# Sums' loads on SP in the order of use, steps that make sums placed anew, and two places of the first feed-forward moved

## The chip, the cores and the metric

The kernel runs on one core of one Trainium2 chip. The metric is the device time of one execution in microseconds. Three runs of the kernel before took 800.18, 800.39 and 802.68 us; the median is 800.39 us. A separate execution was profiled; its own time was 802.45 us, of which the profile's span covers 800.6 us.

## The reference

One residual block over 256 tokens of width 1024, in float32:

```
x = x + 0.5 * rmsnorm(swiglu(rmsnorm(x), ffn1))            # D_FF = 2816
h = rmsnorm(x); project h to q, forget, input, output gate (HGRN2), q, k, v, forget (FoX), 2 gates
A = gated linear recurrence (8 heads);  B = forgetting attention (8 heads)
x = x + rmsnorm((gate_A * (A @ w_a) + gate_B * (B @ w_b)) @ w_out)
x = x + rmsnorm(cross attention of x with 256 memory tokens, 4 heads of 256)
x = x + 0.5 * rmsnorm(swiglu(rmsnorm(x), ffn2))
```

with `swiglu(h) = (silu(h @ w_gate) * (h @ w_up)) @ w_down`. All weights are read once from HBM.

## The kernel before

**Number format.** A float32 operand is split into two parts, hi (a cast to the matmul's float32r format) and lo (the rest), and a product is made of three matmuls: hi by hi, hi by lo, lo by hi. So each weight unit, a tile of 128 x 1024 (512 KB), goes through three queues: a load into one of 4 "raw" buffers, issued by SP (line 137); a cast on ScalarE (ACT, line 138); and a subtraction on VectorE (DVE, line 139). The results lie in 8 "hi" and 8 "lo" buffers until TensorE (PE, line 94) has used them. Other splits go through the helper `split` (lines 157 and 158).

**Order.** The work is written in program order, and a scheduler, whose own estimate of durations is part of the toolchain, gives each engine one fixed order. `after(i)` puts instructions behind the i-th matmul of the list `log`, with high priority; `tc.issue_after(ins)` puts what follows behind `ins` on that engine. Each engine, and SP and GpSimd (POOL) as issuers of DMAs, works through its order one by one: an instruction that waits holds all behind it.

**Feed-forward.** The 2816 hidden columns are 11 chunks of 256 (gate and up together 512 columns wide). Most chunks are made by `act_tok`, 24 matmuls for each half h of 128 tokens. Pairs of chunks at 5 and 8 (first feed-forward) and at 3, 5, 7 and 9 (second) are made by `quad`, a Strassen-like scheme: seven products of half-size blocks in place of eight, which needs sums of blocks of tokens and sums of blocks of weights. `mixed` makes the tokens' sums once for each feed-forward: it adds hi and lo, multiplies with a row of norms (a small matmul behind the last one in `log`, then ACT), splits the product, makes four sums (line 291) and splits these. `down(c, h)` applies w_down to a chunk's activations; `flush` transposes these activations on TensorE ahead of it.

**Sums of weights.** In the first feed-forward `quad` makes them itself (lines 481 to 494). For the second one they are made ahead, during the middle part of the kernel, in 16 steps. A step loads two units (1 MB) into a "wide" buffer by POOL's queue (`load_step`, line 754), makes four sums in place on DVE (`at`, lines 766 to 769), and stores them to a DRAM tensor `sums` by POOL's queue (line 771), after which it loads the next step but one. `SUMS_AT` says behind which stage of the program each step stands; `TO_GATES` is the number of steps that are loaded before the branch gates, which take one of the wide buffers for themselves for a time. There are 2 wide buffers, and they are the same ones into which `sum_of` of the second feed-forward loads finished sums through SP's queue (line 450).

**Middle part.** The stages in order: `i_a`, `f_a`, `q_a`, output gate with FoX forget, `k_b` and `q_b` (the recurrence's levels run beside these), `v_b`, `gates` 0 to 3, `br_a` and `br_b`, `w_out`, `mk`, `mq`, values `mem_v(0)`, the scores and the softmax of the memory attention (lines 1244 to 1264; the transposes of p are line 1264), `mem_v(1)`, `mo`.

Of the kernel before, what the change touches and what calls it, by code (L numbers as in the profile page):

```python
# [31 lines left out]
L_ACT = 21  # L32
# [21 lines left out]
L_MX = 30  # L54

SUMS_AT = (
    ("i_a", 0), ("f_a", 0), ("f_a", 1), ("q_a", 0), ("q_a", 1), ("q_b", 0), ("q_b", 1), ("gates", 2),
    ("br_a", 0), ("br_b", 0), ("br_a", 1), ("br_b", 1), ("mk", 2), ("mk", 3), ("mq", 0), ("mq", 1),
)
TO_GATES = 7  # L60

_ORDER = [
    ("f1_in", 4 * NFF), ("f1_dn", 2 * NFF),
# [5 lines left out]
_AT = {}  # L71
# [8 lines left out]
def block_kernel(ctx: ExitStack, tc: tile.TileContext, wts, head_in, gf_in, x_in, mem_in, memT_in, cols, rows, fbias, masks, out):  # L80
    nc = tc.nc
    V, S, G, PE = nc.vector, nc.scalar, nc.gpsimd, nc.tensor
# [37 lines left out]
    def trp():  # L120
        return pp.tile([P, 512], F32, tag="tr", name=nm("tr"), bufs=2)
# [3 lines left out]
    loads = []  # L125
# [255 lines left out]
    def ffn(w_in, w_dn, X, r2, n_tok, i_row, quads, sums, first_half, second_half=None):  # L381
# [5 lines left out]
        def flush(n):  # L387

            if late:
                c = late.pop(0)  # L390
                tr = trp()
                trv = tr.rearrange("p (j t) -> p j t", j=2)
                with after(n):
                    for h in range(2):
                        for j in range(2):
                            PE.transpose(trv[:, j, h * P : (h + 1) * P], ats[c, h][:, j * P : (j + 1) * P], ident)  # L396
                    split(acts[c][:, 0], acts[c][:, 1], trv)
# [30 lines left out]
        def quad(c, n_down):  # L428
# [12 lines left out]
            if sums:  # L441
                for i in range(4):
                    hi, lo = load_split(wts[_AT[w_in] + 4 * c + i - 4])
                    B11.append((hi[:, :512], lo[:, :512]))
                    B21.append((hi[:, 512:], lo[:, 512:]))

                def sum_of(k):
                    W = wp.tile([P, 2, D], F32, tag="wide", name=nm("wide"), bufs=2)
                    for q in range(2):
                        loads.append(nc.sync.dma_start(W[:, q], sums[c][(0, 3, 2, 1)[k], q]).ins)  # L450
                    return two(W[:, 0].rearrange("p (i n) -> p i n", i=2)) + two(W[:, 1].rearrange("p (i n) -> p i n", i=2))

                def lower():
                    out = []
                    for q in range(2):
                        u = _AT[w_in] + 4 * c + 2 * q
                        raw = wp.tile([P, D], F32, tag="raw", name=nm("raw"), bufs=4).rearrange("p (i n) -> p i n", i=2)
                        loads.append(nc.sync.dma_start(raw, wts[u : u + 2, :, 512:].rearrange("i p n -> p i n")).ins)
                        out += two(raw)
                    return out  # L460

                summed = None
            else:
                wide, made = [], [[], [], []]
                for q in range(2):
                    W = wp.tile([P, 2, 2, 512], F32, tag="wide", name=nm("wide"), bufs=2)
                    raws = []
                    for i in range(2):
                        u = _AT[w_in] + 4 * c + 2 * q + i
                        raw = wp.tile([P, D], F32, tag="raw", name=nm("raw"), bufs=4)  # L470
                        loads.append(nc.sync.dma_start(raw, wts[u - 4]).ins)
                        loads.append(nc.sync.dma_start(W[:, i].rearrange("p j n -> p (j n)"), wts[u]).ins)
                        hi, lo = parts_of()
                        split(hi, lo, raw)
                        B11.append((hi[:, :512], lo[:, :512]))
                        B21.append((hi[:, 512:], lo[:, 512:]))
                        raws.append(raw)
                    wide.append(W)
                    t1, t2, t4 = (m4([P, 2, 512], n="sum") for _ in range(3))
                    for i in range(2):  # L480
                        V.tensor_tensor(out=t1[:, i], in0=raws[i][:, :512], in1=W[:, i, 0], op=ALU.add)
                    V.tensor_tensor(out=t2, in0=t1, in1=W[:, :, 1], op=ALU.add)
                    for i in range(2):
                        summed = V.tensor_tensor(out=t4[:, i], in0=t2[:, i], in1=raws[i][:, 512:], op=ALU.add).ins
                    for k, t in zip((0, 1, 2), (t1, t2, t4)):
                        made[k].append(t)

                def sum_of(k):
                    if k != 2:
                        t = made[min(k, 2)]  # L490
                        return two(t[0]) + two(t[1])
                    out = []
                    for W in wide:
                        V.tensor_tensor(out=W[:, :, 0], in0=W[:, :, 0], in1=W[:, :, 1], op=ALU.add)  # L494
                        out += two(W[:, :, 0])
                    return out

                def lower():
                    return two(wide[0][:, :, 1]) + two(wide[1][:, :, 1])
# [27 lines left out]
            n = len(log)  # L527
# [18 lines left out]
            n = len(log)  # L546
# [8 lines left out]
            n = len(log)  # L555
# [15 lines left out]
            n = len(log)  # L571
# [50 lines left out]
        for c in range(n_tok, NFF):  # L622
            if c in acts:
                continue
            if c in quads:
                quad(c, done)
                done += 2
                continue
            acts[c] = m4([P, 2, 2, T], F32R, "act")
            if quads and c == quads[0] - 1 and c == 2:  # L630
                ready = mixed(X, r2, L_MX)
            if c == 2 and first_half:
                n = len(log)
                outs = act_first(c, mm)
                for h in range(2):
                    flush(n + L_ACT + 24 * h)
                    act_evac(outs[h], c, h)
            else:
                for h in range(2):
                    n = len(log)  # L640
                    act_tok(c, h)
                    if c == 2 or c > NFF - STAG + 1 or c - 2 in quads:
                        flush(n + L_ACT)
            if c == NFF - 1:
                flush(n + L_ACT)
            if quads and c == quads[0] - 3:
                ready = mixed(X, r2)
            if quads and c == max(2, quads[0] - 2):
                mix.append(ready)
                X = ready[0]  # L650
            if grow is None and c >= quads[0] - 1:
                grow = load_row(i_row)
                if first_half:
                    with tc.issue_after(loads[-1]):
                        nc.sync.dma_start(masks_s, masks)
            if accs is None:
                accs = [[acc(), acc()], [acc(), acc()]]
            while done < min(c - 1, NFF - STAG):
                n = len(log)
                for h in range(2):  # L660
                    down(done, h)
                if c + 1 not in quads:
                    flush(n + L_ACT)
                done += 1
# [64 lines left out]
    def half(X, r, h, g, *ms):  # L729

        for i, m in enumerate(ms):
            with after(m):
                to_T(X, x_blocks(h), h, g, (i,) if len(ms) == 2 else (0, 1))
        r[h] = rstd_x(x_halves(h))
# [9 lines left out]
    sums = {c: dp.tile([4, 2, P, D], F32, name=f"sums_{c}") for c in QUADS_2}  # L744
    steps = [(c, q, i) for c in QUADS_2 for q in range(2) for i in range(2)]
    slots = []
    brows = []

    def load_step():
        if len(slots) < len(steps) and (brows or len(slots) < TO_GATES):  # L750
            c, q, i = steps[len(slots)]
            W = wp.tile([P, 2, 2, 512], F32, tag="wide", name=nm("wide"), bufs=2)
            for e in range(2):
                G.dma_start(W[:, e].rearrange("p j n -> p (j n)"), wts[_AT["f2_in"] + 4 * (c + e - 1) + 2 * q + i])
            slots.append(W)

    def at(name, c=0):
# [13 lines left out]
            G.dma_start(sums[u][2 * e : 2 * e + 2, q, :, i * 512 : i * 512 + 512].rearrange("k p n -> p k n"), W[:, e])  # L771
        load_step()

    for _ in range(2):
        load_step()

    iv = [m4([P, 2, 512], n="iv") for _ in range(2)]
    for h in range(2):
        m = len(log)
        for c in range(2):  # L780
            ps = mm()
            proj_tok(ps, X2, chunk("i_a", c), h)
            iv_last = S.activation(iv[c][:, h, :], ps, AF.Copy, scale=r2[h]).ins
        if h == 0:
            half(X2, r2, 1, G_MIX, m + L_IA)
        at("i_a", h)
    row2 = row_of(r2)

# [18 lines left out]
    for c in range(2):  # L807
        u = chunk("f_a", c)
        f, k = m4([P, 4, T], n="f"), m4([P, 4, T], n="k")
# [12 lines left out]
    for c in range(2):  # L822
        u = chunk("q_a", c)
        q = m4([P, 4, T], n="q")
# [111 lines left out]
    for c in range(3):  # L936
        u = [load_split(gf_in[4 * c + i], GF) for i in range(4)]
        n = min(GF, D - c * GF)
# [59 lines left out]
    for h in range(2):  # L998
        ps = [acc(), acc()]
        for hd in range(8):  # L1000
            g, i = hd // 4, hd % 4
# [239 lines left out]
    for h in range(2):  # L1241
# [14 lines left out]
        p = m4([P, 4, T], n="pm")  # L1256
# [140 lines left out]
```

## Time and profile before

| | |
|---|---|
| median of three runs | 800.39 us |
| profiled execution, its own time | 802.45 us |
| its span | 800.6 us |
| TensorE busy | 778.9 us, 97% |
| VectorE busy | 646.0 us, 81% |
| ScalarE busy | 470.2 us, 59% |
| GpSimd busy | 50.1 us, 6% |
| moved by DMA | 193.61 MB, mean 242 GB/s |

How to read the lines below: times are microseconds from the span's start. PE is TensorE's matmul, PEld its weight load, SPq the queue of DMAs that SP issues. `L94` is a line of the kernel; since `MM` records every matmul, they all have that line, and the tiles tell them apart, as `out<-in`: `mm<-hi,hT` is a product of a weight's hi part with the tokens' hi part, `raw<-in_wts_dram` the load of a weight unit, `wide<-in_wts_dram` a step's load, `sums<-wide` its store, `wide<-sums` the load of finished sums. A bracket at the end of a time line's row is the idle time of that engine just before, and what ended it. A row of the waits reads: waiting engine, tile and line, what it waited for, us in total, how often, the longest. A matmul's busy time overlaps with the next one's, so the distance between starts is the rate.

### The profile page before, as it was taken

To read this page: it belongs to the slowest core of one execution; us is meant where nothing else is said; L and a number is where in the kernel's file an instruction comes from. 1 tells how busy PE (TensorE), PEld (TensorE's weight loads), DVE (VectorE), ACT (ScalarE), POOL (GpSimd) and SP (SyncE) were. 2 spreads that over 40 slices of the span, in tenths; PEclk is the share of its full clock that TensorE was granted. 3 is DMA by queue.
4 is the path that set the end of the run, shared out by engine and by line. 5 is a ranking of instruction groups with operands and counts; after the bars stand their busy time and mean duration, and the time that the engine had idled before them with its cause. 6 is when DMAs were issued, how large, how long until landed. Compare 5 with 4: busy or idle time off the path is not lost.

```text
span 800.6 us, 13165 instructions
## 1 busy us (share of the span) xinstructions
PE 778.9 (97%) x5004; PEld 671.3 (84%) x5004; DVE 646.0 (81%) x1004; ACT 470.2 (59%) x704; POOL 50.1 (6%) x85
## 2 busy tenths in 40 slices
PE   9999999999999999999999999999599999999995
PEld 7878888878899989998888888998488888888884
DVE  6898989868788998599686887976566999978864
ACT  7655664656753447249674345652556758777753
POOL 0000000100112200210001211022000000000000
PEclk9999999999999999999999999999799999999998
DMA  9766474674679964865579998578834269989831
GB/s 350 248 220 239 167 289 141 241 249 158 246 254 323 315 228 126 320 208 190 166 263 343 340 353 310 166 254 300 326 118 161 90 204 313 363 309 313 310 106 53
DMA packets 57391, 193.61 MB, mean 242 GB/s; under 512 B 6248, under 2 KB 9712, under 8 KB 57328
## 3 DMA queue, kind: packets, MB, share of 16 engines
q1 hardware_dynamic: 47504, 157.50, 57.4%
q0 software_dynamic: 9680, 35.14, 11.9%
q8 instruction: 39, 0.64, 0.3%
q14 instruction: 24, 0.20, 0.1%
q10 hardware_dynamic: 144, 0.13, 0.0%
HBM read 174.92 MB, written 17.83 MB: 241 GB/s over the span
## 4 chain that ended last, share of the span: by engine, by line
PE 77%; DMA 9%; DVE 8%; ACT 3%; issue 2%; POOL 0%; DVEq 0%; ACTq 0%; POOLq 0%; SPq 0%
PE mm L94 47%; PE acc L94 24%; DMA raw<-in_wts_dram 5%; PE tr L94 3%; DVE lo L139 3%; DMA sums<-wide 2%; ACT hi L138 2%; PE tr L396 1%; PE tr L316 1%; DMA wide<-in_wts_dram 1%; DMA head<-in_head_dram 0%; ACT hT L157 0%; DVE lT L158 0%; PE tr L1264 0%; ACT junk L244 0%
## 5 line engine op out<-in xcount | busy, mean ns | idle before, releaser
L139 DVE TENSOR_TENSOR lo<-raw,hi 128x1024 fp32r<-128x1024 f32 (+1 forms) x228 | 271.0, 1202 | 65.8 <-ACT hi L138 61.6
L138 ACT CAST hi<-raw 128x1024 fp32r<-128x1024 f32 (+1 forms) x228 | 232.8, 1036 | 141.8 <-PE mm L94 67.6
L94 PE MATMUL mm<-hi,hT 128*128 128x512 f32 (+1 forms) x448 | 171.7, 387 | 0.5 <-DVE G L944 0.4
L94 PE MATMUL mm<-lo,hT 128*128 128x512 f32 (+1 forms) x448 | 171.8, 387 | 0.0
L94 PE MATMUL mm<-hi,lT 128*128 128x512 f32 (+1 forms) x448 | 171.4, 387 | 0.0
L94 PE MATMUL acc<-hi,act 128*128 128x512 f32 x352 | 113.2, 391 | 0.7 <-ACT act L157 0.6
L94 PE MATMUL mm<-hT,hi 128*128 128x256 f32 x384 | 109.0, 284 | 0.6 <-DVE zf L946 0.6
L94 PE MATMUL mm<-hT,lo 128*128 128x256 f32 x384 | 109.0, 284 | 0.0
L94 PE MATMUL mm<-lT,hi 128*128 128x256 f32 x384 | 108.9, 284 | 0.0
L94 PEld LDWEIGHTS mm<-hi,hT 128*128 128x128 f32 x448 | 84.7, 189 | 17.2 <-ACT hT L272 0.7
L94 PEld LDWEIGHTS mm<-hi,lT 128*128 128x128 f32 x448 | 84.5, 189 | 15.9 <-DVE lT L273 0.5
L94 PEld LDWEIGHTS mm<-lo,hT 128*128 128x128 f32 x448 | 84.4, 189 | 14.7
L94 PEld LDWEIGHTS acc<-hi,act 128*128 128x128 f32 x352 | 66.0, 188 | 15.3 <-ACT act L157 1.2
L94 PEld LDWEIGHTS mm<-hT,hi 128*128 128x128 f32 x384 | 73.6, 192 | 0.9 <-ACT hi L138 0.8
L94 PEld LDWEIGHTS mm<-lT,hi 128*128 128x128 f32 x384 | 73.6, 192 | 0.2
L94 PEld LDWEIGHTS mm<-hT,lo 128*128 128x128 f32 x384 | 73.6, 192 | 0.1
L94 PE MATMUL acc<-lo,act 128*128 128x512 f32 x176 | 69.2, 393 | 1.3 <-DVE lo L139 1.3
L158 DVE TENSOR_TENSOR lo<-wide,hi 128x1024 fp32r<-128x1024 f32 x40 | 47.7, 1220 | 3.5 <-ACT hi L157 2.9
L157 ACT CAST hi<-wide 128x1024 fp32r<-128x1024 f32 x40 | 41.8, 1053 | 12.2 <-DVE wide L494 3.4
L94 PEld LDWEIGHTS acc<-lo,act 128*128 128x128 f32 x176 | 33.1, 188 | 8.3 <-DVE lo L139 1.8
L771 POOL DMA_DIRECT2D sums<-wide x32 | 23.5, 734 | 243.7 <-DVE wide L768 222.3
L94 PE MATMUL mm<-hi,sh 128*128 128x512 f32 x96 | 37.5, 390 | 0.0
(243 smaller groups left out, 1130.7 us busy)
## 6 DMA issues: line engine op xcount, KB each, us to landing
raw<-in_wts_dram SPq DMA_DIRECT2D x232, 512.0 KB, 4.7
wide<-in_wts_dram POOLq DMA_DIRECT2D x32, 512.0 KB, 6.7
sums<-wide POOLq DMA_DIRECT2D x32, 512.0 KB, 6.1
wide<-sums SPq DMA_DIRECT2D x32, 512.0 KB, 6.0
raw<-in_gf_dram SPq DMA_DIRECT2D x12, 344.0 KB, 4.8
wide<-in_wts_dram SPq DMA_DIRECT2D x8, 512.0 KB, 6.5
head<-in_head_dram SPq DMA_DIRECT2D x8, 388.0 KB, 5.7
grow<-in_rows_dram SPq DMA_DIRECT2D x4, 512.0 KB, 6.1
```

The lines of the kernel that those rows point to most:

```text
L94: log.append(PE.matmul(*args, **kw).ins)
L138: S.copy(h, r)
L139: V.tensor_tensor(out=l, in0=r, in1=h.bitcast(F32), op=ALU.subtract)
L157: S.copy(hi, src)
L158: V.tensor_tensor(out=lo, in0=src, in1=hi.bitcast(F32), op=ALU.subtract)
L316: PE.transpose(ps[:, j * P : (j + 1) * P], src(kb), ident)
L396: PE.transpose(trv[:, j, h * P : (h + 1) * P], ats[c, h][:, j * P : (j + 1) * P], ident)
L771: G.dma_start(sums[u][2 * e : 2 * e + 2, q, :, i * 512 : i * 512 + 512].rearrange("k p n -> p k n"), W[:, e])
```

## The change

Five edits, with no operation added or removed. (1) In `sum_of` of the second feed-forward each load of finished sums is put behind the load that was traced last before it, so that SP's queue has them in program order. (2) The places of the 16 steps in `SUMS_AT` are others, and 6 of them instead of 7 are loaded before the gates. (3) The first two steps' loads are issued by SP instead of POOL, behind the weights of `i_a`, and they are traced after the first half of `i_a` rather than before it. (4) In the first feed-forward `mixed` is traced after chunk 3 instead of chunk 2, and chunk 4 uses the unmixed tokens. In the second one these conditions select the same chunk as before. (5) The flush in the second half of a chunk that follows a pair (chunks 7 and 10 of the first feed-forward) stands behind that half's matmul 12 instead of 21.

```diff
 SUMS_AT = (
-    ("i_a", 0), ("f_a", 0), ("f_a", 1), ("q_a", 0), ("q_a", 1), ("q_b", 0), ("q_b", 1), ("gates", 2),
-    ("br_a", 0), ("br_b", 0), ("br_a", 1), ("br_b", 1), ("mk", 2), ("mk", 3), ("mq", 0), ("mq", 1),
+    ("i_a", 1), ("f_a", 0), ("f_a", 1), ("q_a", 0), ("k_b", 1), ("v_b", 1), ("gates", 1), ("gates", 3),
+    ("br_a", 0), ("br_b", 0), ("br_a", 1), ("br_b", 1), ("mk", 1), ("mk", 3), ("mq", 1), ("mv", 1),
 )
-TO_GATES = 7
+TO_GATES = 6
+L_LAST = 12
...
                 def sum_of(k):
                     W = wp.tile([P, 2, D], F32, tag="wide", name=nm("wide"), bufs=2)
                     for q in range(2):
-                        loads.append(nc.sync.dma_start(W[:, q], sums[c][(0, 3, 2, 1)[k], q]).ins)
+                        with tc.issue_after(loads[-1]):
+                            loads.append(nc.sync.dma_start(W[:, q], sums[c][(0, 3, 2, 1)[k], q]).ins)
...
                     if c == 2 or c > NFF - STAG + 1 or c - 2 in quads:
-                        flush(n + L_ACT)
+                        flush(n + (L_LAST if h and c - 2 in quads else L_ACT))
...
-            if quads and c == quads[0] - 3:
+            if quads and c == quads[0] - 2:
                 ready = mixed(X, r2)
-            if quads and c == max(2, quads[0] - 2):
+            if quads and c == max(2, quads[0] - 1):
                 mix.append(ready)
                 X = ready[0]
...
             for e in range(2):
-                G.dma_start(W[:, e].rearrange("p j n -> p (j n)"), wts[_AT["f2_in"] + 4 * (c + e - 1) + 2 * q + i])
+                part, src = W[:, e].rearrange("p j n -> p (j n)"), wts[_AT["f2_in"] + 4 * (c + e - 1) + 2 * q + i]
+                if len(slots) < 2:
+                    with tc.issue_after(loads[-1]):
+                        nc.sync.dma_start(part, src)
+                else:
+                    G.dma_start(part, src)
             slots.append(W)
...
-    for _ in range(2):
-        load_step()
-
...
         if h == 0:
             half(X2, r2, 1, G_MIX, m + L_IA)
+            for _ in range(2):
+                load_step()
         at("i_a", h)
```

## The prediction

> **What bounds the kernel now.** I read the page first (busy shares and the granted clock), then TensorE's waits, then the time lines around each of them.
>
> ```profile
> span 800.6 us, 13165 instructions
> PE 778.9 (97%) x5004; PEld 671.3 (84%) x5004; DVE 646.0 (81%) x1004; ACT 470.2 (59%) x704; POOL 50.1 (6%) x85
> ```
>
> TensorE is the bound: 778.9 of 800.6 us. Nothing in the diff removes a matmul, so the change can only win what TensorE loses: its waits, and a lower clock. TensorE's waits in full, and four stretches of the windows view (columns: stretch, length, busy time and count of PE, PEld, DVE, ACT and POOL, clock, DMA share, GB/s):
>
> ```profile
> PE tr L1264 <- DVE pm L1260: 9.0, 1, 9.0
> PE acc L94 <- DVE lo L139: 1.3, 1, 1.3
> PE mm L94 <- DVE zf L946: 0.6, 1, 0.6
> PE acc L94 <- ACT act L157: 0.6, 1, 0.6
> PE mm L94 <- DVE G L944: 0.4, 1, 0.4
> PE acc L94 <- DVE act L158: 0.2, 1, 0.2
> ...
> 40.00:60.00 20.00, 18.67 (x85) 15.10 (x84) 18.12 (x26) 11.04 (x15) 0.00 (x0) 1.00 0.65 221
> 60.00:80.00 20.00, 20.00 (x92) 16.49 (x91) 17.14 (x20) 10.18 (x12) 0.00 (x0) 1.00 0.66 238
> ...
> 576.00:582.00 6.00, 6.00 (x21) 5.00 (x20) 2.92 (x5) 3.95 (x11) 0.00 (x0) 0.57 0.19 79
> ...
> 680.00:700.00 20.00, 19.92 (x92) 16.22 (x91) 18.59 (x21) 14.95 (x19) 0.00 (x0) 1.00 0.96 367
> ```
>
> The waits sum to 12.1 us. The 9.0 us one is in the memory attention, and right after it the clock is 0.57 for 6.0 us, worth (1 - 0.57) x 6.0 = 2.6 us more. So at most about 14.7 us can be won. Why that wait is there, in the time lines of SP, POOL, ACT and DVE (start, duration, what; idle before and its releaser in brackets):
>
> ```profile
> 534.22 9.03 SPq L137 DMA_DIRECT2D raw<-in_wts_dram  x4
> 554.81 0.33 SPq L450 DMA_DIRECT2D wide<-sums  x1
> 555.25 1.85 SPq L137 DMA_DIRECT2D raw<-in_wts_dram  x4
> ...
> 547.73 1.46 POOL L771 DMA_DIRECT2D sums<-wide  x2 [0.26 <-issue]
> ...
> 560.11 1.05 ACT L138 CAST hi<-raw 128x1024 fp32r<-128x1024 f32 x1 [8.04 <-DMA raw<-in_wts_dram]
> ...
> 547.14 2.51 DVE L139 TENSOR_TENSOR lo<-raw,hi 128x1024 fp32r<-128x1024 f32 x2 [0.45 <-ACT hi L138]
> 552.30 0.69 DVE L766 TENSOR_TENSOR wide<-wide 128x512 f32<-128x512 f32 x1 [2.06 <-DMA wide<-in_wts_dram]
> 567.08 1.23 DVE L139 TENSOR_TENSOR lo<-raw,hi 128x1024 fp32r<-128x1024 f32 x1 [1.26 <-ACT hi L138]
> 568.88 0.74 DVE L1254 TENSOR_REDUCE mx<-acc 128x1 f32<-128x256 f32 x2
> ...
> 566.25 0.39 PE L94 MATMUL mm<-hi,lT 128*128 128x512 f32 x1
> 575.64 1.94 PE L1264 MATMUL tr<-ident,pm 128*128 128x128 f32 x8 [9.00 <-DVE pm L1260]
> ```
>
> SP issues nothing between 543.3 and 554.8. At its head stands a load of finished sums for the second feed-forward (wide<-sums); it waits for a "wide" buffer, which comes free when the stores that POOL issued at 547.73 have landed. Four loads of weights are stuck behind it. Their casts start at 560.11 after 8.04 us of waiting, their third split at 567.08; ACT and DVE run in order, so the softmax stands behind them: first reduction at 568.88, transposes at 575.64. TensorE had run out at 566.6.
>
> **The change, part by part.**
>
> *Order of the sums' loads (sum_of).* No instruction more or less; each such load may be issued on SP only after the last load traced before it. The one at 554.81 then stands behind the weights of the memory attention. The four stuck loads need only raw buffers, which DVE frees by splits: the two from 547.14 had ended by 549.65, and the next was held only by the 2.06 us wait for a step's load, in a step that the new spread moves. So the weights come some 5 to 8 us sooner. Where does the softmax then stand? The scores are 48 matmuls (2 halves, 4 heads, 2 blocks, 3 products):
>
> ```profile
> 562.25 0.28 PE L94 MATMUL acc<-hT,lT 128*128 128x256 f32 x1
> 562.37 0.40 PE L94 MATMUL mm<-hi,hT 128*128 128x512 f32 x1
> ```
>
> They start every 0.12 us (562.25 to 562.37), so the first half's 24 end 24 x 0.12 = 2.9 us ahead of 562.4, at 559.5. From first reduction to transposes it was 575.64 - 568.88 = 6.8 us, which gives 566.3, against 566.6 when TensorE runs out. Lower bound of the rest wait: 0. Upper bound: 9.0, if the chain is late for another reason. I take 1.0, near the lower end, since the four casts (1.05 each) may still fall into the chain. **-8.0.** A rest of 1 us leaves the clock alone: the stretch 40 to 60, with the 1.3 us wait in it (20.00 - 18.67), has clock 1.00. **-2.6.** The Trainium skill (TensorE: Matmul & The Clock Gate, What's actually happening) has the clock halved after an idle window of about 3.4 us; by it the 2.6 us come back only if more than about 3.4 us of the wait stay, and the sum would then be that of the first rival below; no run here shows a gap between 1.3 and 9.0 us.
>
> What the order costs: the first quad of the second feed-forward finds its first two sums no longer loaded ahead.
>
> ```profile
> 652.11 7.23 SPq L137 DMA_DIRECT2D raw<-in_wts_dram  x5
> ...
> 658.90 2.35 DVE L158 TENSOR_TENSOR lo<-wide,hi 128x1024 fp32r<-128x1024 f32 x2
> ...
> 662.68 0.40 PE L94 MATMUL mm<-hi,sh 128*128 128x512 f32 x1
> ...
> wide<-sums SPq DMA_DIRECT2D x32, 512.0 KB, 6.0
> ```
>
> The fourth weight of that quad is issued at 652.11, so its sums follow at about 652.5 and 652.9 and land near 659 (6.0 us). A cast and a split (1.05 + 1.22) end near 661.3, where the split at 658.90 ended too; TensorE wants it at 662.68. Bounds: 0, and 6.0 when a whole landing is exposed. I take **+0.4**, near 0, since 1.4 us are to spare. Later quads:
>
> ```profile
> 698.50 1.44 SPq L137 DMA_DIRECT2D raw<-in_wts_dram  x2
> 699.99 0.42 SPq L450 DMA_DIRECT2D wide<-sums  x1
> ```
>
> Here the order is already nearly that of use. Cost 0, hidden by the splits that run ahead; without that cover it is the slower rival below.
>
> *Tokens' sums one chunk later (mixed).* Its DVE work, by group, in 38 to 60, and the first quad's second sum:
>
> ```profile
> L282 DVE TENSOR_TENSOR full<-full,row 128x1024 f32<-128x1024 f32 x2 | 2.4, 1223 | 0.3 <-ACT row L264 0.3
> L158 DVE TENSOR_TENSOR sl<-sums,sh 128x1024 fp32r<-128x1024 f32 x2 | 2.4, 1224 | 0.6 <-ACT sh L157 0.6
> L291 DVE TENSOR_TENSOR sums<-full 128x256 f32<-128x256 f32 x4 | 1.5, 419 | 0.0
> ...
> 90.11 1.22 DVE L158 TENSOR_TENSOR lo<-sum,hi 128x1024 fp32r<-128x1024 f32 x1
> ...
> 91.75 0.39 PE L94 MATMUL mm<-hi,sh 128*128 128x512 f32 x1
> ```
>
> That is 2.4 x 3 + 1.5 x 2 = 10.2 us behind the row (the pair lT has the shape of the pair sl; four more forms besides the four shown), which moves behind chunk 3's matmuls, most of it into 60 to 80. In its place the weights' splits come forward, up to the 8 hi/lo buffers: seven of 1.2 us, 8.4. The 1.3 us wait, for such a split, goes: **-1.3**. Net DVE has 1.8 us more to do there ahead of the first quad, against 20.00 - 17.14 = 2.9 us idle in 60 to 80. Late next would be the quad's second sum, split at 91.3, wanted at 91.75 (0.4 us to spare). Bounds 0 and about 5 (10.2 less 2.9, 0.4 and 1.9, if only a part of the splits, 1.9 us of them, comes forward); I take 0, since the idle time covers the net.
>
> *Flush at matmul 12 instead of 21 (L_LAST).* One place counts, chunk 10: the waits 0.6 (act L157) and 0.2 (act L158) are for transposes queued after 21 of the chunk's 24 matmuls, whose casts the next product needs at once. Nine matmuls earlier is 9 x 20.00 / 92 = 2.0 us: **-0.8**, bounds 0 and -0.8.
>
> *First loads later.* Four issues of 512 KB leave POOL at 148.93 for SP, behind the input projection's weights; 2 MB (5.7 us at the 367 GB/s of 680 to 700) then stand ahead of the next weights on SP.
>
> ```profile
> 148.93 2.31 POOL L754 DMA_DIRECT2D wide<-in_wts_dram  x4 [147.61 <-DVE lo L158]
> ...
> 184.34 29.48 SPq L137 DMA_DIRECT2D raw<-in_wts_dram  x11
> ...
> 203.18 1.06 ACT L138 CAST hi<-raw 128x1024 fp32r<-128x1024 f32 x1 [0.15 <-PE mm L94]
> ```
>
> The weight behind them, the third of those eleven issues and by an estimate at 190 (184.34 + 2 x 29.48 / 10), is cast only at 203.18, when TensorE frees a buffer; of these 13 us a landing as long as the sums' 6.0 leaves 7 to cover 5.7. Without that cover it costs up to 5.7. I take 0; POOL, idle there, wins nothing by it.
>
> *Steps spread anew.* The same 16 steps (four DVE operations, two stores and two loads each). One leaves the stretch that ends at 268 (q_a, 1), two stand among the gates where one stood, the last moves into the values' projection; on POOL each keeps its stores behind its sums and its loads behind the stores' landing.
>
> ```profile
> 267.68 1.46 POOL L771 DMA_DIRECT2D sums<-wide  x2 [4.89 <-DVE G L944]
> ```
>
> DVE is rid of 4 x 0.69 = 2.8 us (a step's operation is the one at 552.30) and DMA of 1 MB of stores, in the stretch ahead of the 0.4 and 0.6 us waits for G and zf, which DVE serves in order. Bounds 0 and -1.0; I take **-0.6**. From the gates on, one step more than before is still to do: 2 MB more of DMA there, 5.7 us if all of it delayed weights, 0 if they run ahead by more; TensorE shows no wait there now, so **+0.3**.
>
> Sum: -8.0 - 2.6 - 1.3 - 0.8 - 0.6 + 0.4 + 0.3 = **-12.6**. The profiled execution took 802.45 us, 2.06 above the median of the three (800.39): 789.85 against its own, **787.8** against the median.
>
> **The rivals** (times against the median).
> *Half the wait stays*, 4.5 us, and the clock falls as it did after 9.0: only 4.5 + 1.3 + 0.8 + 0.6 - 0.7 = 6.5 are won: 793.9. For it: ACT and DVE orders are fixed ahead of time and may put casts before the softmax. Against: casts then don't wait.
> *The first quad of the first feed-forward starves*, 5 us by the bound above: 792.8.
> *It doesn't do what it says*: another load heads SP's queue, or the softmax is late by itself; of the gains 1.3 + 0.8 stay, less 0.7: 799.0, within 0.3% (798.0 to 802.8, about what a measurement here can tell from no change).
> *Slower:* in the second feed-forward, loads of sums in order stand behind weights that wait for raw buffers, and one landing (6.0 us) is exposed in each of four quads: +24 - 12.6 = 811.8. It decides from 12.6 / 4 = 3.2 us a quad. Against: the rows at 698.50 and 699.99 already have that order, and no wait there stands among TensorE's.
>
> **How the numbers follow.** Forecast 0.60 (784 to 792); half 0.13; starving 0.08; no effect 0.09; slower 0.10. Faster 0.81, same 0.09, slower 0.10. The range 783 to 797.5 holds the first three; 800.4 - 14.7 = 785.7 is all the waits won at no cost, and 783 leaves 2.7 for steps too short for the list of waits.
>
> **What would show it.** The wait of tr L1264 on pm under 2 us and clock 1.00 at 576 to 582; SP issuing weights all through 543 to 555, wide<-sums first at about 650; no waits for lo L139, act L157 and act L158 as listed above; no new wait of mm on lo L158 near 91.75 or after 650. It is wrong if the softmax still waits with weights on time, or if quads wait for sums.

## The result and the profile after

The changed kernel takes 789.62 us (median of four runs, 787.73 to 790.70) against 800.28 us for the kernel before (median of four runs beside it): a ratio of 0.9865, 95% interval 0.9828 to 0.9901. The profiled execution took 789.21 us, 13.2 less than the 802.45 us of the one before.

First the page of the changed kernel:

```profile
span 787.1 us, 13170 instructions
PE 775.7 (99%) x5004; PEld 670.5 (85%) x5004; DVE 646.0 (82%) x1004; ACT 469.5 (60%) x704; POOL 48.6 (6%) x81
```

Then all of TensorE's waits in it, from the view of waits:

```profile
PE tr L93 <- DVE ones L206: 1.1, 1, 1.1
PE tr L93 <- DVE ct L1030: 1.0, 1, 1.0
PE tr L315 <- DVE lT L272: 0.9, 1, 0.9
PE acc L93 <- issue: 0.4, 1, 0.4
```

All six waits that the prediction listed (12.1 us) are gone. The rows for ones and issue are no news: the kernel before had them too (1.1 and 0.3 us), so the prediction was wrong to call its list of waits full. New are the waits for ct and lT, together 1.9 us. With the clock's 2.6 us that makes -12.1 - 2.6 + 1.9 = -12.8 us, of the 13.2 between the two profiled executions.

The stretch that had the low clock before, in the windows view, and then the softmax, which now comes some 10 us sooner, in the time lines of the changed kernel:

```profile
576.00:582.00 6.00, 5.91 (x40) 5.16 (x40) 4.93 (x8) 3.36 (x6) 0.00 (x0) 1.00 0.60 180
```

```profile
538.29 21.35 SPq L136 DMA_DIRECT2D raw<-in_wts_dram  x10
...
557.42 0.74 DVE L1258 TENSOR_REDUCE mx<-acc 128x1 f32<-128x256 f32 x2
...
562.80 1.22 DVE L1264 TENSOR_TENSOR pm<-pm,sm 128x1024 f32<-128x1024 f32 x1
...
565.55 1.03 PE L1268 MATMUL tr<-ident,pm 128*128 128x128 f32 x8
```

SP issues weights in the stretch in which it stood still before; between 536 and 562 it still waits 18.8 us in all for DVE to free raw buffers, but no longer for a buffer of sums. The first reduction is at 557.42 (568.88 before), pm is done at 564.02, and the transposes' row has no idle time ahead of it; the clock is 1.00 from 555 to 582.

### The profile page after: what moved, and what is told of

It is laid out like the page before. It is cut to its first block, busy times and chain, and to the rows that moved or that the text cites. A ratio compares the mean times of both kernels' runs of the same rounds, so it can differ in the third digit from the quotient of the medians.

```text
span 787.1 us, 13170 instructions
## 1 busy us (share of the span) xinstructions
PE 775.7 (99%) x5004; PEld 670.5 (85%) x5004; DVE 646.0 (82%) x1004; ACT 469.5 (60%) x704; POOL 48.6 (6%) x81
## 4 chain that ended last, share of the span: by engine, by line
PE 96%; DVE 1%; DMA 1%; ACT 1%; issue 1%; DVEq 0%; ACTq 0%
PE mm L93 62%; PE acc L93 27%; PE tr L93 4%; PE tr L395 1%; DMA raw<-in_wts_dram 1%; PE tr L315 1%; PE tr L1069 0%; ACT hi L137 0%; PE tr L1161 0%; PE tr L1268 0%; DVE lo L138 0%; ACT L357 0%; DVE y L229 0%; DVE t L227 0%; PE tr L406 0%
## 5 line engine op out<-in xcount | busy, mean ns | idle before, releaser
L157 DVE TENSOR_TENSOR lo<-wide,hi 128x1024 fp32r<-128x1024 f32 x40 | 48.0, 1219 | 2.0 <-ACT hi L156 1.4
```

The costliest lines, as they stand in the source:

```text
L157: V.tensor_tensor(out=lo, in0=src, in1=hi.bitcast(F32), op=ALU.subtract)
```

## The experiments

Times of one group were taken on one chip, beside runs of the kernel before there (medians 801.13, 801.74, 801.66 and 801.74 us in the four groups). Ratios are against these.

### Which edit won the score wait

**The first edit alone, on the kernel before** (`sum_of`):

```diff
                     for q in range(2):
-                        loads.append(nc.sync.dma_start(W[:, q], ...).ins)
+                        with tc.issue_after(loads[-1]):
+                            loads.append(nc.sync.dma_start(W[:, q], ...).ins)
```

> The kernel before with the first edit alone: each load of finished sums stands on SP behind the load traced last before it. Theory (this edit wins the 9.0 us wait and the 2.6 us of clock): SP issues weights all through 543 to 555, the transposes of pm wait at most 1 us, the clock is 1.00 from 576 to 582; the waits of 1.3 (lo), 0.6 (zf), 0.6 and 0.2 (act) and 0.4 us (G) stay. 800.3 - 11.6 + 0 to 1 = 788.7 to 789.7 us. Rival (the weights come sooner only because the spread moves the step at 552.30, for whose load DVE waited 2.06 us): more than half of the wait stays, 4.5 us and the clock with it, 793 to 797 us.

792.94 us (791.26 to 796.51), ratio 0.9897 (0.9853 to 0.994). The wait of the scores among its TensorE waits:

```profile
PE tr L1265 <- DVE pm L1261: 0.3, 1, 0.3
```

On the wait the theory held: it is 0.3 us, and the clock from 560 to 582 is 1.00. So the edit is enough to win it. The time is above the 788.7 to 789.7 us of the theory: two runs took 791.3 us, the other two 794.6 and 796.5, near the rival's times. The trace, in which nothing of the score wait is left, is of a run of 791.26 us; what the longer ones lost is not known, and neither is whether this edit alone is worth less than the others.

**The changed kernel without it:**

> The changed kernel without the first edit. Its first two loads of finished sums then stand some seven places later on SP than in the kernel before, just ahead of the load of grow, which the changed kernel issues at 559.70, and the next two some ten places further. Theory A (the order edit is what wins the score wait): the wait is back, 9.0 + 2.6 us: 789.6 + 11.6 = 801 us. Theory B (the spread alone already takes the load from the head of SP's queue while the scores' weights are issued): the score wait stays away; the next two loads wait for the last step's stores (issued at 583.43, about 6 us to land) and hold weights until about 590, at most 5 us of new wait near 590 to 600: 789.6 to 795 us.

788.91 us, ratio 0.984 (0.9807 to 0.9874): not slower than with it. Theory A fell. Two of its four waits (the others are issue and ones), then SP's time line:

```profile
PE tr L315 <- DVE lT L272: 1.3, 2, 1.0
...
PE tr L93 <- DVE ct L1029: 1.0, 1, 1.0
```

```profile
536.62 21.08 SPq L136 DMA_DIRECT2D raw<-in_wts_dram  x9
557.87 0.33 SPq L449 DMA_DIRECT2D wide<-sums  x1
```

A load of finished sums stands on SP among the weights here too, but behind the nine issued from 536.62 on, at 557.87; in the kernel before it came right behind the four issued from 534.22 on, and SP stood still until 554.81. The next pair, at 590.68, held nothing that TensorE waited for, so the 5 us that theory B allowed for it did not come.

**The second and third edits alone, on the kernel before:**

> The kernel before with the second and third edits alone (the places of the steps, six of them before the gates, the first two steps' loads on SP). Theory A (the order edit is needed): the score wait of about 9 us and the low clock stay, 800 +- 2 us. Theory B (the spread alone is enough): the wait is gone, the 1.3, 0.6 and 0.2 us waits of the first feed-forward stay, and the two new waits of the changed kernel (1.0 at ct, 0.9 at lT) are here too: 800.3 - 11.6 - 1.0 + 1.9 = 789.6, up to 5 us more if later weights are held behind sums' loads, 789 to 795 us.

790.90 us, ratio 0.9869 (0.9835 to 0.9902): theory B. There is no wait for pm and none for G or zf, while the waits for ct (1.0) and lT (1.5 in all) are here.

**The places of the last two steps alone, on the kernel before:**

```diff
-    ("br_a", 0), ("br_b", 0), ("br_a", 1), ("br_b", 1), ("mk", 2), ("mk", 3), ("mq", 0), ("mq", 1),
+    ("br_a", 0), ("br_b", 0), ("br_a", 1), ("br_b", 1), ("mk", 2), ("mk", 3), ("mq", 1), ("mv", 1),
```

> The kernel before with the places of its last two steps alone changed, from behind mq (first and second) to behind mq (second) and the values' second half. Theory (what the new spread does to the score wait is that the wide buffer comes free later, so that the first load of finished sums gets a later place on SP, behind the scores' weights): the score wait of 9.0 us and the low clock are gone, all else is as in the kernel before: 801.1 - 11.6 = 789.5 us, with the waits of up to 1 us at 268 to 295 and in the first feed-forward still there, up to 792. Rival (other steps of the spread are needed): the wait stays above 4.5 us, 796 to 801 us.

789.47 us, ratio 0.9838 (0.9818 to 0.9857): as fast as the whole change. Its waits and SP's time line:

```profile
PE acc L94 <- ACT act L157: 1.3, 1, 1.3
PE tr L94 <- DVE ones L207: 1.1, 1, 1.1
PE mm L94 <- DVE zf L946: 0.6, 1, 0.6
PE mm L94 <- DVE G L944: 0.3, 1, 0.3
PE acc L94 <- DVE act L158: 0.2, 1, 0.2
```

```profile
533.31 23.64 SPq L137 DMA_DIRECT2D raw<-in_wts_dram  x11
558.82 0.33 SPq L450 DMA_DIRECT2D wide<-sums  x1
```

What SP waited for between 540 and 562 at the load of finished sums, in the kernel before and then in this one:

```profile
SPq L450 <- DMA sums<-wide: 11.3, 1, 11.3
```

```profile
SPq L450 <- DMA sums<-wide: 1.6, 1, 1.6
```

There are two things to see. The load of sums holds SP only from 556.95 (533.31 + 23.64) to 558.82, after eleven weights instead of four. Its buffer does not come free sooner: the stores that it waits for leave POOL at 552.15 here and at 547.73 before. It is the later place in the queue that helps, as with the first edit. And the small waits of the kernel before (act, zf, G) are still here, while those for ct and lT are not: what the whole change wins with its other edits it about loses again at ct and lT.

### The two edits of the first feed-forward

The fourth edit undone in the changed kernel, and then the fifth (`L_LAST = 21`):

> The changed kernel with the tokens' sums of the first feed-forward made after chunk 2 again. Theory: the 1.3 us wait for lo near 50 us is back and nothing else changes: 789.6 + 1.3 = 790.9 us. Rival (the flush or the spread took this wait, not the place of the sums): no such wait, 789.6 us. The trace decides, since 1.3 us is near what the times can tell.

> The changed kernel with the flush of the fifth edit behind matmul 21 again. Theory (this place, and nothing else of the change, took the waits for act): a wait of 0.2 to 1.3 us for act near 171 is back, the spread of the runs that kept the old place (0.8, 1.7, 0.2 and 1.5 us in all); 790.0 + 0.8 = 790.8 us. Rival (the waits for act went because weights come otherwise ahead of 171): no such wait, 790.0 us. The trace decides.

789.69 us, ratio 0.9852 (0.9813 to 0.989), and 790.17 us, ratio 0.9852 (0.9814 to 0.989): neither differs from the changed kernel by more than the runs scatter. One row of the waits of each:

```profile
PE acc L93 <- DVE lo L138: 0.7, 1, 0.7
```

```profile
PE acc L93 <- ACT act L156: 0.2, 1, 0.2
```

Each wait is back, smaller than before (1.3 and 0.6). They vary between kernels that have the same code there, each profiled once: with the tokens' sums in the old place the wait for lo was 1.3 us before, 0.7 here, and absent in the three kernels above made from the kernel before; with the old flush the wait for act L157 was 0.6 before, 1.2, 0.2 and 1.3 in those three. With the new places neither was seen in any run. So the edits remove these waits, and are worth 0 to 1.3 us (lo) and 0.2 to 1.7 us (the two for act together); the times cannot show it.

### The two new waits

> The changed kernel again, beside the next two on one chip. 789.6 us, waits of about 1.0 us (ct) near 347 and 0.9 to 1.3 us (lT) near 380, no score wait.

790.28 us, ratio 0.9865 (0.9843 to 0.9888), with waits of 0.9 us for ct and 2.9 us for lT: 1.6 us in two near 376 to 380, and one of 1.3 us in another stretch (near 512), which no run explains.

The wait for ct in the changed kernel, time lines of POOL and DVE:

```profile
335.62 1.46 POOL L776 DMA_DIRECT2D sums<-wide  x2 [31.73 <-DVE wide L774]
337.08 1.12 POOL L1021 DMA_DIRECT2D cbm<-cd  x2
344.69 2.74 POOL L1023 TENSOR_SCALAR_AFFINE_SELECT cbm<-cbm 128x1024 f32<-128x1024 f32 x2 [6.49 <-DMA cbm<-cd]
...
344.83 1.04 DVE L227 SCALAR_TENSOR_TENSOR t<-v,y 128x1 f32<-128x1 f32 x1
345.80 0.68 DVE L772 TENSOR_TENSOR wide<-wide 128x512 f32<-128x512 f32 x1
346.40 1.04 DVE L229 SCALAR_TENSOR_TENSOR y<-t,y 128x1 f32<-128x1 f32 x1
347.36 0.16 DVE L1030 COPY ct<-tr 128x16 f32<-128x16 f32 x1
```

The stores of the step behind k_b wait for DVE, and the loads of cbm, which are queued behind them on POOL, are issued at 337.08 (at 327.04 before). So POOL's two affine_selects fall at 344.69. Two operations on 128 x 1 elements beside them took 1.04 us each, and the second ended with the selects (346.40 + 1.04 = 347.44, 344.69 + 2.74 = 347.43); ct stands behind them. **Only these stores moved**, behind the selects (the diff is shortened, with remarks added):

```diff
-        for e in range(2):
-            G.dma_start(sums[u]...)          # at the step
+        held.append(stores)                  # the step behind k_b (the second) only
...
         cbm.append(t)
+    with tc.issue_after(sel):                # sel: the last affine_select
+        held.pop()()
```

> The changed kernel with one thing moved: on POOL the two stores of the step behind k_b (the second) stand behind the two affine_selects instead of ahead of the loads of cbm. Every instruction of the other engines stays in its place. Theory (the small operations of the rstd chain at 344.83 and 346.40 took 1.05 us each because DVE and POOL cannot run such a pair at once, and POOL's affine_selects came beside them only because the stores held the loads of cbm up): the selects come some 8 us sooner, the same small operations take 0.15 to 0.22 us, the wait for ct is gone: 789.6 - 1.0 = 788.6 us; the lT wait near 380 stays. Rival (these operations are slow for another reason, such as the step's additions on DVE beside them): they stay at 1.05 us and the wait of 1.0 us stays: 789.6 us.

788.10 us, ratio 0.9836 (0.9813 to 0.9858). The same operations, with the selects gone to 324.04 and 326.53:

```profile
343.78 0.21 DVE L227 SCALAR_TENSOR_TENSOR t<-v,y 128x1 f32<-128x1 f32 x1
343.91 0.68 DVE L773 TENSOR_TENSOR wide<-wide 128x512 f32<-128x512 f32 x1
344.51 0.15 DVE L229 SCALAR_TENSOR_TENSOR y<-t,y 128x1 f32<-128x1 f32 x1
344.58 0.17 DVE L1039 COPY ct<-tr 128x16 f32<-128x16 f32 x1
```

They took 0.21 and 0.15 us, still beside the step's additions, so the rival fell; the wait for ct is gone and that for lT (1.1) stays.

**Both steps behind q_b, seven steps loaded ahead of the gates:**

```diff
-    ("i_a", 1), ("f_a", 0), ("f_a", 1), ("q_a", 0), ("k_b", 1), ("v_b", 1), ("gates", 1), ("gates", 3),
+    ("i_a", 1), ("f_a", 0), ("f_a", 1), ("q_a", 0), ("q_b", 0), ("q_b", 1), ("gates", 1), ("gates", 3),
...
-TO_GATES = 6
+TO_GATES = 7
```

> The changed kernel with the fifth and sixth steps behind q_b (first and second) as in the kernel before, and seven steps loaded ahead of the gates. Theory: the step's additions no longer lie inside the softmax of the forgetting attention, its stores and the next load (364 to 369) no longer fall on the weights' loads at 366 to 370, so both new waits go, ct 1.0 and lT 0.9 to 1.3: 789.6 - 2.1 = 787.5 us. Rival (the lT wait comes from elsewhere): it stays, 788.6 us. If the step put back ahead of 350 costs what it did before, waits up to 1.0 us at 268 to 295 do not come back, since that step is not there.

788.16 us, ratio 0.9838 (0.9816 to 0.986). lT does not wait any more, but ct does (1.1), against the expectation. POOL and DVE there:

```profile
345.23 3.20 POOL L1023 TENSOR_SCALAR_AFFINE_SELECT cbm<-cbm 128x1024 f32<-128x1024 f32 x2 [10.22 <-DMA cbm<-cd]
...
345.91 1.57 DVE L772 TENSOR_TENSOR wide<-wide 128x512 f32<-128x512 f32 x1
...
347.57 1.40 DVE L773 TENSOR_TENSOR wide<-wide 128x512 f32<-128x512 f32 x1
```

The seventh step's load now holds POOL's queue until its buffer is free (331.63), the loads of cbm follow at 333.96, and the selects are late again. This time they fall on the step's additions, which take 1.57 and 1.40 us in place of 0.68.

**Both mended** (the diff of the places alone): the stores behind k_b after the selects, the sixth step behind q_b (second) with its stores after the selects too, six steps ahead of the gates as in the change:

```diff
-    ... ("q_a", 0), ("k_b", 1), ("v_b", 1), ("gates", 1), ...
+    ... ("q_a", 0), ("k_b", 1), ("q_b", 1), ("gates", 1), ...
```

> The changed kernel with the stores behind k_b moved behind the affine_selects, and with the sixth step behind q_b (second) instead of the values' projection, its stores too behind the selects. Theory: no wait for ct, and the sixth step's transfers fall some 15 us sooner, ahead of the weights' loads at 366 to 370, so the lT wait near 380 (1.1 us beside the moved stores alone) goes too: 788.1 - 1.1 = 787.0 us. Rival (the lT wait is that of ACT's order, not of the transfers): it stays, 788.1 us.

785.87 us (785.09 to 786.65), ratio 0.9797 (0.9782 to 0.9811): faster than both kernels, since its slowest run is below the fastest of the changed one (787.73). Its waits:

```profile
PE tr L93 <- DVE ones L206: 1.1, 1, 1.1
PE acc L93 <- issue: 0.8, 1, 0.8
PE tr L315 <- DVE lT L272: 0.3, 1, 0.3
```

The wait for lT near 380 is gone too; the 0.3 us that is left lies between 500 and 510. Why lT waited near 380 shows in the changed kernel's time lines of ACT and POOL and, in two stretches, in its windows; the fence after that has the windows of the mended kernel:

```profile
377.55 1.05 ACT L137 CAST hi<-raw 128x1024 fp32r<-128x1024 f32 x1 [0.53 <-DMA raw<-in_wts_dram]
...
364.23 0.74 POOL L776 DMA_DIRECT2D sums<-wide  x1 [14.89 <-DVE wide L774]
368.62 1.11 POOL L759 DMA_DIRECT2D wide<-in_wts_dram  x2 [3.66 <-DMA sums<-wide]
```

```profile
350.00:364.00 14.00, 14.00 (x63) 11.70 (x64) 13.74 (x43) 7.35 (x27) 0.00 (x0) 1.00 0.13 51
...
370.00:380.00 10.00, 9.03 (x43) 6.91 (x42) 7.74 (x15) 7.99 (x16) 0.00 (x0) 1.00 1.01 360
```

```profile
350.00:364.00 14.00, 14.00 (x65) 11.68 (x64) 12.54 (x38) 7.95 (x28) 1.12 (x2) 1.00 0.36 134
...
370.00:380.00 10.00, 10.00 (x50) 8.08 (x49) 9.25 (x19) 8.22 (x19) 0.00 (x0) 1.00 0.94 302
```

The step behind v_b had its last addition inside the softmax of the forgetting attention, so its second store left at 364.23 and the next load at 368.62, just when weights were wanted: DMA share 0.13 ahead of that and 1.01 behind it. ACT's cast then waited for its weight, and lT, which stands behind the cast, came 0.9 us too late for TensorE. With the step earlier, 10 of 10 us are busy. The edit moves the step's additions on DVE as well as its transfers; that the transfers count rests on the cast's wait for its load.

### What a pause of TensorE costs beyond itself

The changed kernel with pauses ahead of gate projections, made by a chain of DVE operations that one added transpose, and the products behind it, wait for:

> The changed kernel with two pauses of TensorE put in: ahead of the third and of the fourth gate projection a chain of DVE operations (2 and 4 of 128 x 512, about 0.7 us each) must end before one added transpose and all that projection's matmuls. Idle windows of about 2.5 and 4 to 5 us. If the clock falls after windows over about 3.4 us only (the figure of the Trainium skill, TensorE: Matmul & The Clock Gate, What's actually happening), the first leaves the clock at 1.00 and the second brings it near 0.57 for some 5.6 us as the 9.0 us window did: 789.6 + 2.5 + 4.5 + 2.4 = 799.0 us. Rival: both keep 1.00, 796.6 us; or both lose it, 801.4 us.

> The changed kernel with two shorter pauses of TensorE, ahead of the second half of the third and of the fourth gate projection, of 1 and 2 DVE operations; windows of about 2.2 and 3 to 4 us by the pauses measured before (5.6 and 5.5 us, both with the clock at 0.56 to 0.61 in the five us behind them). If windows under about 3.4 us leave the clock alone, the first is followed by 1.00; if every pause of over 2 us halves it, both are followed by about 0.6. Time 789.6 + 2.2 + 3.5 and 0, 2.4 or 4.8 for the clock: 795.3 to 800.1 us.

The first took 805.65 us, the second 798.76 us, one run each. The pauses came out longer than meant, since DVE had other work in its order: 5.5 and 5.6 us, then 3.9 and 2.3 us. Windows of the first kernel behind its second pause, and of the second behind its 3.9 us and its 2.3 us pause:

```profile
432.00:438.20 6.20, 5.98 (x15) 4.76 (x16) 0.08 (x1) 0.00 (x0) 0.00 (x0) 0.52 0.48 164
438.20:445.00 6.80, 6.80 (x31) 5.62 (x30) 2.46 (x3) 2.32 (x3) 0.00 (x0) 1.00 0.00 0
```

```profile
418.00:422.20 4.20, 3.71 (x11) 3.03 (x12) 1.86 (x10) 0.67 (x1) 0.19 (x1) 0.60 0.73 270
422.20:430.00 7.80, 7.80 (x36) 6.42 (x36) 5.47 (x5) 4.61 (x5) 1.11 (x2) 1.00 0.73 272
433.00:440.00 7.00, 6.68 (x30) 5.58 (x31) 3.74 (x4) 4.01 (x4) 0.00 (x0) 1.00 0.43 148
```

2.3 us leave the clock at 1.00; 3.9 and 5.6 us do not. What follows at the lower clock is 3 to 6 us long; by these windows it costs, as an estimate, (1 - 0.60) x 4.2 = 1.7 us after the 3.9 us pause and (1 - 0.52) x 6.2 = 3.0 us after the 5.6 us one. The Trainium skill (TensorE: Matmul & The Clock Gate, What's actually happening) has the limit at about 3.4 us; these pauses lie on both sides of it and agree.

## Why the prediction was right, and where not

- **Size and sign** were right: 787.8 us forecast, 789.62 measured; the sum -12.6 against the profiled time, -13.2 measured. Part of that agreement is luck, since misses of both signs cancel.
- **Order of the sums' loads, -8.0.** The mechanism (a load at the head of SP's queue that waits for a buffer, weights behind it, softmax behind their casts) held. The rest wait was 0 instead of the 1.0 taken, so the term was -9.0. What failed is the credit: the step gave the whole gain to the edit in `sum_of`, and treated the spread as a help to it. The runs show that either is enough for this wait, and that of the spread the places of the last two steps do it alone; beside the spread, the edit in `sum_of` won nothing that the times show (788.91 us without it). The clue stood in the code: the load waits for the buffer of one of the last steps, and where those steps move, the scheduler gives the load a later place.
- **Clock, -2.6**: right. The rival "half the wait stays" took the clock to fall after 4.5 us as after 9.0; the pause of 3.9 us bears that out.
- **First quad of the second feed-forward, +0.4, and later quads, 0**: nothing was lost. The first load of sums was issued at 639.88, not near 652.5: it has to follow only the loads traced before it. The slower rival, one landing exposed a quad, did not appear in any kernel that had the order.
- **Tokens' sums later, -1.3 and 0**: the wait for lo went and no quad starved, though DVE was busy 20.00 of the 20 us from 60 to 80. The price was taken from one execution of a wait that ranges from 0 to 1.3.
- **Flush, -0.8**: gone as forecast; by the runs 0.2 to 1.7 for the two act rows together, again a wait that varies.
- **First loads later, 0**: right; no wait of TensorE near 190 to 205.
- **Steps spread, -0.6**: both waits for G and zf went, -1.0, the bound.
- **From the gates on, +0.3**: mis-sized; the mechanism, a step's megabytes ahead of weights, is the lT wait near 380, 0.9 us in one execution and 1.6 in the next.
- **Missing**: the 1.0 us for ct. The part on POOL's queue said that each step "keeps its stores behind its sums and its loads behind the stores' landing", but did not name what else stands on that queue: the loads of cbm, and behind them the affine_selects.

## What to carry to other kernels

When a queue's head waits for a buffer, look at who frees that buffer as well as at the order of the queue: here moving the steps that free it gave the load a later place as well, and so cleared the same stall, and two edits that each clear it do not add up. Where a step is moved, list every instruction of every in-order queue that it comes to stand ahead of, loads and POOL operations included. A small wait seen in one profiled execution is worth a range from zero to its size until a second execution shows it again.

## What the runs showed of the hardware

An operation of DVE on 128 x 1 elements with two inputs in SBUF took 1.04 us instead of 0.15 to 0.21 while POOL ran an affine_select of 128 x 1024, and an addition of 128 x 512 took up to 1.57 instead of 0.68; an operation without a second tensor input inside a select (v<-ss at 347.44 in the kernel with seven steps loaded ahead) took 0.21 us, as elsewhere. The selects themselves took 1.09 us in the kernel before and 1.53 and 1.71 us beside these additions. The Trainium skill (SBUF — State Buffer, SBUF: two separate sides) has DVE and POOL share a pair of ports that the one that starts first holds for its whole instruction, against a DVE operation with two inputs in SBUF too; the trace agrees, down to the small operation that ends with the select. So in these traces even an operation of 0.15 us took as long as what was left of the select.

What stays open: a wait put down to issue, near 268 to 276 at a product of the recurrence, was 0.4 us in the changed kernel and up to 2.2 in the others, and no run tells what it is. A wait for hT of 0.2 to 1.0 us, in the first 9 us of five of the kernels, is not explained either.
